# Summing the indexer's head scores on TensorE with diagonal weight matrices, and moving half of the queries behind the second selection

## Chip, cores and metric

The kernel runs on one core of one Trainium2 chip. The metric is the device time of one execution in microseconds (us); smaller is better. The inputs are float32, one sequence of 256 tokens of width 1024.

## What is computed

The program is a two-layer decoder trunk. Layer 0 uses a sparse latent attention: a small "indexer" scores every key for every query, the 64 best keys are kept, and eight heads attend over them. Layer 1 uses another attention (compressed blocks, selected blocks, a sliding window). Each layer ends in an MLP of width 4096. The change lies in the indexer and the attention of layer 0 alone:

```python
c_q, c_kv, k_idx, w_idx = split(h @ w_in, ...)         # 256, 128, 64, 8 columns; the first three normalised
q     = einsum('btr,rhd->bthd', c_q, w_uq)             # 8 heads of 128
q_abs = einsum('bthd,chd->bthc', q, w_uk) * HEAD_DIM ** -0.5
q_idx = einsum('btr,rhd->bthd', c_q, w_q_idx)          # 8 index heads of 64
rel   = relu(einsum('bqhd,bsd->bqhs', q_idx, k_idx))   # per index head
score = einsum('bqh,bqhs->bqs', w_idx, rel)            # weighted sum over the index heads
score = where(key_pos <= t, score, NEG)
_, sel = top_k(score, 64)
logits = einsum('bqhc,bqkc->bqhk', q_abs, c_kv[sel]) + rel_bias[...]
o_lat  = einsum('bqhk,bqkc->bqhc', softmax(logits), c_kv[sel])
```

## The kernel before

The 256 queries are two blocks of 128, `i` = 0 and 1. Block 0 sees 128 keys, block 1 sees 256. Queries lie on the 128 partitions, keys along the free dimension.

- **Index scores (lines 385 to 412).** `index_scores(i, m0)` multiplies the indexer's queries by the keys on TensorE in float32, two heads for each `m`, and ScalarE applies the relu into `rels[i]`.
- **Sum over heads (lines 461 to 466).** `score(i, n)` is one VectorE instruction: `rel` of head `n` times the head's weight `widx` (one value per query) plus the running sum. The first one adds the causal mask `cmask`. Eight of them make the score of one block.
- **Selection (lines 470 to 484).** `top8` finds the eight largest values of each row, `drop8` replaces them by a sentinel. Eight rounds of both mark 64 keys, and `select(i)` turns the marks into an additive mask `selm[i]`. All of these are VectorE instructions in an order written out by hand (`dve` is `inorder`, which puts each one behind the one before it on its engine).
- **Queries (lines 428 to 445).** `queries(hp)` makes the queries of a pair of heads. Each product is three TensorE passes over operands that are split into a high and a low half in fp32r (`mm3`); the halves of the weights are `wuq[j]`, where `j` = 0 holds heads 0 to 3 and `j` = 1 heads 4 to 7. The high half is a cast on ScalarE, the low half a subtraction on VectorE (line 379). `absorbed(hp)` multiplies by `w_uk` in float32.
- **Logits (lines 492 to 506).** `logits(i, h0)` computes two or four heads in one PSUM bank. `masked` adds `selm[i]` through a matmul with the identity, into the same bank. `exps`, `norms`, `transposed`, `values` and `upv` make the softmax and the mix; `wo_head` adds one head of the output projection `ya`.
- **Order.** The text of lines 677 to 772 gives the order in which work is issued. A scheduler may move an instruction ahead of others on its engine when its operands are ready; `pin` keeps an instruction in the order of the text, `behind` ties it to another one. Engine queues run in order. `Pieces` cuts a GpSimd operation into pieces of 256 columns and gives each piece an order; `load_wo(None, 0, 1)` loads the first two heads' output weights on the SP queue and splits them on GpSimd.
- **Buffers.** PSUM has two pools of four banks: `acc` (projections, logits, `ya`) and `ps` (everything else). `bigt` takes one of ten 8 KB slots per partition.

Of the kernel before, what the change touches and what calls it, by code (L numbers as in the profile page):

```python
# [22 lines left out]
F32 = mybir.dt.float32  # L23
F32R = mybir.dt.float32r
AF = mybir.ActivationFunctionType
OP = mybir.AluOpType
# [4 lines left out]
P, T, D, KT = 128, 256, 1024, 8  # L31
H, G, R, HD = 8, 2, 4, 128
# [18 lines left out]
def trunk(ctx: ExitStack, tc: tile.TileContext, I, out):  # L51
    nc = tc.nc
# [17 lines left out]
    def bank(name, acc=False):  # L70
        if acc:
            return psA.tile([P, 512], F32, tag="acc", name=name)
        return psB.tile([P, 512], F32, tag="ps", name=name)

    def bigt(shape, dt, name):
        return big.tile(shape, dt, tag="big", name=name)

    def wk(tag, bufs, shape, name, dt=F32):
        return work.tile(shape, dt, tag=tag, name=name, bufs=bufs)
# [10 lines left out]
    def f(ap):  # L90
        return ap.bitcast(F32)

    def mm(ps, a, b, start, stop):
        return nc.tensor.matmul(ps, a, b, start=start, stop=stop, skip_group_check=True)  # L94

    def mm3(ps, ah, al, bh, bl, start, stop):
        mm(ps, ah, bh, start, False)
        mm(ps, ah, bl, False, False)
        mm(ps, al, bh, False, stop)

    def behind(ins, prev):

        tc.add_manual_dep(ins.ins, prev.ins.name,
                          mybir.DependencyInfo(mybir.DependencyClass.NoSync, mybir.DependencyReason.DATA),
                          reason="order")
# [42 lines left out]
    def colw(src, name, m=P, lo=None, after=None, hi=None):  # L148
        h, l = weights(src, name, lo, after, hi)
        return (h.rearrange("p (k m) -> p k m", m=m), l.rearrange("p (k m) -> p k m", m=m))  # L150

    def pin(ins):

        return tc.keep_in_program_order(ins)
# [95 lines left out]
    for j in range(4):  # L250
# [8 lines left out]
        else:  # L259
            xh = nc.scalar.copy(xgh[:, pair], xT[:, pair])  # L260
            nc.vector.tensor_sub(xgl[:, pair], xT[:, pair], f(xgh[:, pair]))
            w = wp.tile([P, 2, 1024], F32R, tag="w", name=f"win{j}")
            wh, wl = (w[:, s, :912].rearrange("p (a m) -> p a m", a=2) for s in range(2))
            for a in range(2):
# [3 lines left out]
                                                         op0=OP.mult, op1=OP.subtract)  # L268
# [15 lines left out]
    ident = cst[:, C_ID:C_ID + P]  # L284
    cmask = cst[:, C_CM:C_CM + T]
# [8 lines left out]
    wuqr = [rawp.tile([P, 1024], F32, tag="raw", name=f"wuqr{j}") for j in range(2)]  # L294
# [45 lines left out]
    widx = const.tile([P, 2, H], F32, name="widx")  # L340
# [16 lines left out]
    sc = [scs[:, i] for i in range(2)]  # L357
    indexer_queries(0)
    tk = bank("tk")
    for i in range(2):  # L360
        kd = wk("kd", 2, [P, 2, 64], "kd")
        nc.vector.tensor_scalar(kd, proj[i][:, None, 384:448].to_broadcast([P, 2, 64]), sc[i][:, 2:3], None,
                                op0=OP.mult)
        pin(nc.tensor.transpose(tk[:, i * P:(i + 1) * P], kd.rearrange("p a b -> p (a b)"), ident))
    for a in range(2):
        pa = slice(64 * a, 64 * (a + 1))
        kiT_last = nc.vector.tensor_scalar(kiT[pa, a], tk[pa, :T], vec[pa, V_GKI:V_GKI + 1], None, op0=OP.mult)
    indexer_queries(1)
    for i in range(2):
        nc.vector.tensor_scalar(widx[:, i], proj[i][:, 448:456], sc[i][:, 3:4], float(8 ** -0.5 * 64 ** -0.5),  # L370
                                op0=OP.mult, op1=OP.mult)
        nc.vector.tensor_scalar(widx[:, i], widx[:, i], sc[i][:, 0:1], None, op0=OP.mult)
    wuq = []
    for j in range(2):
        w = wp.tile([P, 2, 1024], F32R, tag="w", name=f"wuq{j}")
        cast = nc.scalar.copy(w[:, 0], wuqr[j])
        behind(cast, cqu_last)
        behind(cast, ss_last)
        behind(nc.vector.tensor_sub(w[:, 1], wuqr[j], f(w[:, 0])), kiT_last)
        wuq.append((w[:, 0], w[:, 1]))  # L380


    rels = [bigt([P, 4, 2, (i + 1) * P], F32, f"rel{i}") for i in range(2)]

    def index_scores(i, m0):

        ns = (i + 1) * P
        per = 256 // ns
        ps = bank(f"ix{i}{m0}")
        for m in range(m0, m0 + per):  # L390
            for j in range(2):
                o = ((m - m0) * 2 + j) * ns
                pin(mm(ps[:, o:o + ns], qiT[:, m, i * P:(i + 1) * P], kiT[:, j, :ns], o == 0, o + ns == 512))
        return nc.scalar.activation(rels[i][:, m0:m0 + per].rearrange("p m j s -> p (m j s)"), ps, AF.Relu)
# [11 lines left out]
    for a in range(2):  # L406
# [1 line left out]
        nc.scalar.activation(cqs[:, 0, a], tn[:, a * T:(a + 1) * T], AF.Copy, scale=g)  # L408
        nc.vector.scalar_tensor_tensor(cqs[:, 1, a], tn[:, a * T:(a + 1) * T], g, f(cqs[:, 0, a]),
                                       op0=OP.mult, op1=OP.subtract)  # L410
    for m in range(4):
        rel_last = index_scores(1, m)
    tc_ = bank("tc")
    for i in range(2):
        nc.scalar.activation(ckv[:, i], proj[i][:, 256:384], AF.Copy, scale=sc[i][:, 1:2])
# [12 lines left out]
    def queries(hp):  # L428
        ps = bank(f"q{hp}")
        for a in range(2):  # L430
            h = 2 * hp + a
            for k in range(2):
                c = slice(k * 512 + (h % 4) * P, k * 512 + (h % 4 + 1) * P)
                wh, wl = wuq[h // 4]
                mm3(ps[:, a * T:(a + 1) * T], wh[:, c], wl[:, c], cqs[:, 0, k], cqs[:, 1, k],
                    k == 0 and a == 0, k == 1)
        qt_last.append(nc.scalar.copy(qT[:, 2 * hp:2 * hp + 2].rearrange("p a t -> p (a t)"), ps))

    def absorbed(hp):
        ps = bank(f"qa{hp}")  # L440
        for a in range(2):
            h = 2 * hp + a
            mm(ps[:, a * T:(a + 1) * T], wuk[:, h * P:(h + 1) * P], qT[:, h], a == 0, a == 1)
        qa_last.append(nc.scalar.activation(qabs[:, 2 * hp:2 * hp + 2].rearrange("p a t -> p (a t)"), ps, AF.Copy,
                                            scale=gkvs[:, 0:1]))
# [11 lines left out]
    dve = inorder  # L457

    scores = [wk("sq", 2, [P, T], f"score{i}") for i in range(2)]

    def score(i, n):
        ns = (i + 1) * P
        m, j = divmod(n, 2)
        prev = cmask[:, T - ns:] if n == 0 else scores[i][:, :ns]
        return dve(nc.vector.scalar_tensor_tensor(scores[i][:, :ns], rels[i][:, m, j], widx[:, i, n:n + 1], prev,
                                                  op0=OP.mult, op1=OP.add))

    m8s = {}

# [22 lines left out]
    def logits(i, h0, acc, first=False):  # L492
        ns = (i + 1) * P
        per = 512 // ns
        lg = bank(f"lg{i}{h0}", acc=acc)
        lg3 = lg.rearrange("p (a b) -> p a b", b=ns)
        for h in range(h0, h0 + per):
            ins = mm(lg3[:, h - h0], qabs[:, h, i * P:(i + 1) * P], ckvT[:, :ns], h == h0, False)
            if first and h == h0:
                pin(ins)  # L500
        return lg3

    def masked(i, lg3):
        ns = (i + 1) * P
        pin(mm(lg3, identr, selm[i][:, None, :ns].to_broadcast([P, 512 // ns, ns]), False, True))
        return lg3
# [144 lines left out]
    lg = {}  # L651
    wo = [None] * H

    def load_wo(prev, *hs):
        for h in hs:
            wo[h] = colw(I["a_w_o"][h], f"wo{h}", lo=pieces if h < 6 else nc.vector,
                         after=(prev,) if prev else None, hi=None if prev else pieces.tensor_copy)

    def past(prev):
        return lambda ins: after_sync(ins, prev)  # L660
# [13 lines left out]
        values(i, h0, pT[i, h0], ordered)  # L674


    for n in range(8):
        score(0, n)
    queries(0)
    queries(1)  # L680
    absorbed(0)
    absorbed(1)
    lg[0, 0] = logits(0, 0, True)
    for n in range(4):
        score(1, 2 * n)
        top8(0)
        score_last = score(1, 2 * n + 1)
        drop8(0)
    pieces = Pieces(past(score_last))
    queries(2)  # L690
    queries(3)
    for n in range(4):
        top8(1)
        top8(0)
        drop8(1)
        drop8(0)
    select(0)
    masked(0, lg[0, 0])
    load_wo(None, 0, 1)
    absorbed(2)  # L700
    absorbed(3)
    lg[0, 4] = logits(0, 4, True)
    masked(0, lg[0, 4])
    for h0 in (0, 2):
        lg[1, h0] = logits(1, h0, True, True)
    ex = exps(0, 0, True)
    for rnd in range(4):
        top8(1)
        if rnd in (1, 2):
            ex.pop(0)()  # L710
        drop8(1)
        if rnd in (1, 2):
            ex.pop(0)()
    select(1)
    for h0 in (0, 2):
        masked(1, lg[1, h0])
    lg[1, 4] = logits(1, 4, True, True)
    masked(1, lg[1, 4])
    def run(steps):
        for step in steps:  # L720
            step()
# [12 lines left out]
    pieces = Pieces(past(chains[mybir.EngineType.DVE][-1]))  # L734
# [44 lines left out]
    for fi in range(NF):  # L779
# [8 lines left out]
        if fi == 14:  # L788


            ps = bank("m1_ps")
# [41 lines left out]
    for k in range(KT):  # L833
# [5 lines left out]
        if k == 4:  # L839
            ms2 = small([P, 2], "ms2")  # L840
            ps = bank("ms2_ps")
# [30 lines left out]
    for kv in range(2):  # L872
        ps = bank(f"kc{kv}")
        for g in range(G):
# [4 lines left out]
        ins = nc.vector.tensor_tensor(ff[:, :, :32].rearrange("p b (g c) -> p b g c", g=G),  # L879
                                      ps.rearrange("p (g c b) -> p b g c", g=G, b=16),  # L880
                                      Rb.rearrange("p (c b) -> p b c", b=16)[:, :, None, :].to_broadcast([P, 16, G, 16]),
                                      op=OP.mult)
# [71 lines left out]
    for i in range(2):  # L954
        nc.scalar.activation(Vs[:, 0, i], vps[i], AF.Copy, scale=r2[:, i:i + 1])
        nc.vector.scalar_tensor_tensor(Vs[:, 1, i], vps[i], r2[:, i:i + 1], f(Vs[:, 0, i]),
                                       op0=OP.mult, op1=OP.subtract)
    gk = hidden(0, csk)
    kcT = const.tile([P, 32], F32, name="kcT")
    ps = bank("kcT_ps")  # L960
# [9 lines left out]
    w = wp.tile([P, 2, 1024], F32R, tag="w", name="wg")  # L970
# [190 lines left out]
    ps = bank("vc_ps")  # L1161
# [5 lines left out]
    for a in range(2):  # L1167
# [3 lines left out]
                                       op0=OP.mult, op1=OP.subtract)  # L1171
# [40 lines left out]
    for fi in range(NF):  # L1212
# [14 lines left out]
        if 16 <= fi < 20:  # L1227
            i, c = divmod(fi - 16, 2)
            ps = bank(f"x3t{i}{c}")
# [19 lines left out]
    for i in range(2):  # L1249
        for c in range(2):  # L1250
# [5 lines left out]
            if c == 0:  # L1256
                ins = nc.gpsimd.tensor_tensor(xg[:, i], x4[:, i, :512], gf[:, 0, :512], op=OP.mult)
# [4 lines left out]
        else:  # L1262
            for n in range(2):
                d = slice(512 + 256 * n, 768 + 256 * n)
                ps = bank(f"y11{n}")
# [121 lines left out]
```

## Time and profile before

| what | value |
|---|---|
| median of three runs | 593.86 us (593.1 to 595.12) |
| the profiled execution | 593.29 us |
| span of its trace | 591.5 us |
| PE busy | 577.2 us, 98% |
| PEld (weight loads) busy | 542.9 us, 92% |
| DVE busy | 364.2 us, 62% |
| ACT busy | 320.4 us, 54% |
| POOL busy | 159.1 us, 27% |

PE is TensorE's matmuls, PEld its weight loads (they overlap the matmuls), DVE is VectorE, ACT is ScalarE, POOL is GpSimd. The busy shares are means over the whole span. Matmuls are pipelined and the ends in the trace are modelled, so a busy PE can still have small holes between its instructions. The span is shorter than the time of the execution by what lies ahead of the first and behind the last instruction.

### The profile page before, as it was taken

How to read it: one execution, taken by the hardware profiler on the slowest of the kernel's cores; microseconds unless marked ns; L12 is line 12 of the kernel's file. 1: busy time of each engine (PE TensorE's matmuls, PEld its weight loads, DVE VectorE, ACT ScalarE, POOL GpSimd, SP SyncE). 2: the span in 40 equal slices, each digit the busy share in tenths (PEclk: the TensorE clock that was granted, in tenths of full speed). 3: DMA queues.
4: the chain of work that ended last, by engine and by line, in shares of the span. 5: the costliest groups of instructions: out<-in, count | busy, mean ns of one | idle time of the engine just before them, and what ended most of it. 6: DMA issues, size and time to landing. Idle time of an engine off the chain costs nothing.

```text
span 591.5 us, 10852 instructions
## 1 busy us (share of the span) xinstructions
PE 577.2 (98%) x4170; PEld 542.9 (92%) x4170; DVE 364.2 (62%) x612; ACT 320.4 (54%) x580; POOL 159.1 (27%) x225
## 2 busy tenths in 40 slices
PE   8899999999999999999999999999999999999995
PEld 6787899999999999999968999999899999999994
DVE  3897399544474444547897877639845444454523
ACT  6656666444444454436866878637544545454423
POOL 0155457010101011015530076808310110011012
PEclk9999999999999999999999999999999999999998
DMA  8911447765546656543499943314866665656201
GB/s 300 345 47 61 149 176 235 249 194 178 179 145 212 181 178 190 180 164 113 160 308 304 327 139 102 97 49 138 287 205 186 181 191 169 180 180 203 77 0 71
DMA packets 30475, 103.97 MB, mean 176 GB/s; under 512 B 3632, under 2 KB 5464, under 8 KB 30296
## 3 DMA queue, kind: packets, MB, share of 16 engines
q1 hardware_dynamic: 30024, 102.45, 53.7%
q10 hardware_dynamic: 400, 0.83, 0.5%
q8 instruction: 32, 0.52, 0.4%
q14 instruction: 19, 0.16, 0.1%
HBM read 102.21 MB, written 1.06 MB: 175 GB/s over the span
## 4 chain that ended last, share of the span: by engine, by line
PE 84%; DVE 9%; issue 2%; DMA 2%; ACT 1%; POOL 1%; SPq 1%; POOLq 0%; ACTq 0%; DVEq 0%
PE y L94 30%; PE u L94 28%; PE nq L94 4%; PE yb L94 3%; PE ya L94 3%; PE kk L94 2%; PE npo L94 2%; PE kc L94 1%; PE nl L94 1%; DVE c L903 1%; DMA win_raw<-in_a_w_in 1%; PE v L94 1%; PE co L94 1%; PE ix L94 1%; DMA wv_raw<-in_kvV 1%
## 5 line engine op out<-in xcount | busy, mean ns | idle before, releaser
L142 DVE TENSOR_TENSOR dn<-dn_raw,dn 128x1024 fp32r<-128x1024 f32 x64 | 80.6, 1260 | 99.2 <-ACT dn L141 99.2
L645 POOL TENSOR_TENSOR us<-ur 128x256 f32<-128x256 f32 x64 | 45.4, 711 | 282.0 <-ACT ur L642 282.0
L142 DVE TENSOR_TENSOR up<-up_raw,up 128x1024 fp32r<-128x1024 f32 x64 | 81.9, 1280 | 44.6 <-ACT up L141 44.6
L141 ACT CAST up<-up_raw 128x1024 fp32r<-128x1024 f32 x64 | 67.0, 1048 | 60.0 <-PE y L94 58.5
L94 PE MATMUL u<-h1h,up 128*128 128x256 f32 x512 | 97.0, 284 | 0.6 <-DVE up L142 0.6
L94 PE MATMUL y<-uu,dn 128*128 128x256 f32 x768 | 97.0, 283 | 0.3 <-DVE uu L647 0.3
L94 PE MATMUL u<-h0h,up 128*128 128x256 f32 x512 | 96.7, 283 | 0.0
L94 PEld LDWEIGHTS y<-uu,dn 128*128 128x128 f32 x768 | 94.2, 192 | 0.5 <-DVE uu L647 0.5
L94 PE MATMUL y<-dn,uu 128*128 128x512 f32 (+1 forms) x396 | 92.5, 384 | 0.0
L94 PEld LDWEIGHTS y<-dn,uu 128*128 128x128 f32 x396 | 71.1, 189 | 13.0
L94 PEld LDWEIGHTS u<-h1h,up 128*128 128x128 f32 x512 | 81.5, 191 | 1.6 <-DVE up L142 0.8
L642 ACT ACTIVATE ur<-u 128x256 f32<-128x256 f32 x64 | 24.6, 384 | 107.2 <-PE u L94 107.2
L94 PEld LDWEIGHTS u<-h0h,up 128*128 128x128 f32 x512 | 81.7, 192 | 0.0
L94 PE MATMUL u<-h1l,up 128*128 128x256 f32 x256 | 72.5, 283 | 0.0
L94 PE MATMUL u<-h0l,up 128*128 128x256 f32 x256 | 72.2, 283 | 0.0
L141 ACT CAST dn<-dn_raw 128x1024 fp32r<-128x1024 f32 x64 | 66.7, 1042 | 7.2 <-PE y L94 3.0
L94 PEld LDWEIGHTS u<-h1l,up 128*128 128x128 f32 x256 | 49.0, 191 | 0.9
L94 PEld LDWEIGHTS u<-h0l,up 128*128 128x128 f32 x256 | 49.1, 192 | 0.0
L647 DVE TENSOR_TENSOR uu<-us,uu 128x256 fp32r<-128x256 f32 x64 | 29.1, 455 | 8.1 <-POOL us L645 8.1
L646 ACT ACTIVATE uu<-ur 128x256 fp32r<-128x256 f32 x64 | 26.7, 417 | 0.1
L94 PE MATMUL ya<-oT,wo 128*128 128x256 f32 x192 | 25.2, 288 | 0.3 <-DVE oT L591 0.3
L94 PE MATMUL nq<-ah,wq 128*128 128x256 f32 x128 | 24.9, 286 | 0.0
(300 smaller groups left out, 966.8 us busy)
## 6 DMA issues: line engine op xcount, KB each, us to landing
up_raw<-in_w_up SPq DMA_DIRECT2D x64, 512.0 KB, 3.7
dn_raw<-in_w_down SPq DMA_DIRECT2D x64, 512.0 KB, 3.7
c1raw<-in_cmp_w SPq DMA_DIRECT2D x16, 512.0 KB, 4.9
wo_raw<-in_a_w_o SPq DMA_DIRECT2D x8, 512.0 KB, 4.1
wq_raw<-in_b_w_q SPq DMA_DIRECT2D x8, 512.0 KB, 5.9
wn_raw<-in_b_w_o SPq DMA_DIRECT2D x8, 512.0 KB, 4.9
wk_raw<-in_kvT SPq DMA_DIRECT2D x4, 512.0 KB, 3.6
wc_raw<-in_kvT SPq DMA_DIRECT2D x4, 512.0 KB, 3.6
```

Source lines behind the costliest of these rows:

```text
L94: return nc.tensor.matmul(ps, a, b, start=start, stop=stop, skip_group_check=True)
L141: ins = [hi(w[:, 0, :C], raw[:, :C]) if hi else nc.scalar.copy(w[:, 0, :C], raw[:, :C]), (lo or nc.vector).tensor_sub(w[:, 1, :C], raw[:, ...
L142: (lo or nc.vector).tensor_sub(w[:, 1, :C], raw[:, :C], f(w[:, 0, :C]))]
L642: nc.scalar.activation(r, ps[:, :T], AF.Relu)
L645: nc.gpsimd.tensor_tensor(s, r, r, op=OP.mult)
L646: nc.scalar.activation(u[:, 0], r, AF.Square)
L647: nc.vector.tensor_sub(u[:, 1], s, f(u[:, 0]))
L903: lo = nc.vector.tensor_sub(w4[:, :, 1], r4, f(w4[:, :, 0]))
```

## The change

The sum over the index heads becomes eight matmuls for each block. GpSimd builds `dg`, a 128x128 diagonal matrix for each block and head with the head's weights on the diagonal. `head_sums(i)` multiplies each by `rels[i]` of that head, in float32, and accumulates in one PSUM bank. `score(i)` is then one VectorE addition of the causal mask. The matmuls are pinned in between the index scores of block 1.

The order behind them changes too. `score(1)` stands behind three selection rounds of block 0. The logits of block 1 for heads 0 to 3 are written ahead of the selection; the queries, absorbed queries and logits of heads 4 to 7 stand behind the second selection. The low half of `wuq[1]` is subtracted on GpSimd, behind the diagonal matrices, and the first two output heads' weights are split behind that.

```diff
--- before.py
+++ after.py
@@ -376,8 +376,14 @@
         cast = nc.scalar.copy(w[:, 0], wuqr[j])
         behind(cast, cqu_last)
         behind(cast, ss_last)
-        behind(nc.vector.tensor_sub(w[:, 1], wuqr[j], f(w[:, 0])), kiT_last)
+        if j == 0:
+            behind(nc.vector.tensor_sub(w[:, 1], wuqr[j], f(w[:, 0])), kiT_last)
         wuq.append((w[:, 0], w[:, 1]))
+
+    dg = bigt([P, 2, H, P], F32, "dg")
+    for i in range(2):
+        dg_last = nc.gpsimd.tensor_tensor(dg[:, i], ident[:, None, :].to_broadcast([P, H, P]),
+                                          widx[:, i, :, None].to_broadcast([P, H, P]), op=OP.mult)
 
 
     rels = [bigt([P, 4, 2, (i + 1) * P], F32, f"rel{i}") for i in range(2)]
@@ -408,8 +414,19 @@
         nc.scalar.activation(cqs[:, 0, a], tn[:, a * T:(a + 1) * T], AF.Copy, scale=g)
         nc.vector.scalar_tensor_tensor(cqs[:, 1, a], tn[:, a * T:(a + 1) * T], g, f(cqs[:, 0, a]),
                                        op0=OP.mult, op1=OP.subtract)
-    for m in range(4):
-        rel_last = index_scores(1, m)
+    def head_sums(i):
+        ns = (i + 1) * P
+        ps = bank(f"sc{i}")
+        for n in range(H):
+            pin(mm(ps[:, :ns], dg[:, i, n], rels[i][:, n // 2, n % 2], n == 0, n == H - 1))
+        return ps
+
+    index_scores(1, 0)
+    index_scores(1, 1)
+    sums = [head_sums(0)]
+    index_scores(1, 2)
+    index_scores(1, 3)
+    sums.append(head_sums(1))
     tc_ = bank("tc")
     for i in range(2):
         nc.scalar.activation(ckv[:, i], proj[i][:, 256:384], AF.Copy, scale=sc[i][:, 1:2])
@@ -458,12 +475,9 @@
 
     scores = [wk("sq", 2, [P, T], f"score{i}") for i in range(2)]
 
-    def score(i, n):
+    def score(i):
         ns = (i + 1) * P
-        m, j = divmod(n, 2)
-        prev = cmask[:, T - ns:] if n == 0 else scores[i][:, :ns]
-        return dve(nc.vector.scalar_tensor_tensor(scores[i][:, :ns], rels[i][:, m, j], widx[:, i, n:n + 1], prev,
-                                                  op0=OP.mult, op1=OP.add))
+        return dve(nc.vector.tensor_tensor(scores[i][:, :ns], sums[i][:, :ns], cmask[:, T - ns:], op=OP.add))
 
     m8s = {}
 
@@ -674,48 +688,47 @@
         values(i, h0, pT[i, h0], ordered)
 
 
-    for n in range(8):
-        score(0, n)
+    score(0)
+
+    pieces = Pieces(lambda ins: behind(ins, dg_last))
+    pieces.tensor_sub(wuq[1][1], wuqr[1], f(wuq[1][0]))
+    load_wo(None, 0, 1)
     queries(0)
     queries(1)
     absorbed(0)
     absorbed(1)
     lg[0, 0] = logits(0, 0, True)
-    for n in range(4):
-        score(1, 2 * n)
+    for h0 in (0, 2):
+        lg[1, h0] = logits(1, h0, True)
+    for n in range(3):
         top8(0)
-        score_last = score(1, 2 * n + 1)
         drop8(0)
-    pieces = Pieces(past(score_last))
-    queries(2)
-    queries(3)
-    for n in range(4):
+    score(1)
+    for n in range(5):
         top8(1)
         top8(0)
         drop8(1)
         drop8(0)
     select(0)
     masked(0, lg[0, 0])
-    load_wo(None, 0, 1)
-    absorbed(2)
-    absorbed(3)
-    lg[0, 4] = logits(0, 4, True)
-    masked(0, lg[0, 4])
-    for h0 in (0, 2):
-        lg[1, h0] = logits(1, h0, True, True)
     ex = exps(0, 0, True)
-    for rnd in range(4):
+    for rnd in range(3):
         top8(1)
-        if rnd in (1, 2):
+        if rnd:
             ex.pop(0)()
         drop8(1)
-        if rnd in (1, 2):
+        if rnd:
             ex.pop(0)()
     select(1)
     for h0 in (0, 2):
         masked(1, lg[1, h0])
-    lg[1, 4] = logits(1, 4, True, True)
-    masked(1, lg[1, 4])
+
+    queries(2)
+    queries(3)
+    absorbed(2)
+    absorbed(3)
+    lg[0, 4] = masked(0, logits(0, 4, True))
+    lg[1, 4] = masked(1, logits(1, 4, True))
     def run(steps):
         for step in steps:
             step()
```

## Rows read from the trace of the kernel before

**Rows 1.** Busy by stretch: PE, PEld, DVE, ACT, POOL; then PEclk, DMA share, GB/s.
```profile
22.10:44.81 22.71, 21.86 (x138) 19.38 (x139) 22.20 (x86) 13.39 (x30) 8.49 (x17) 1.00 0.41 135
44.81:53.92 9.11, 8.47 (x39) 6.26 (x39) 5.61 (x23) 6.82 (x21) 3.18 (x9) 1.00 0.10 40
53.92:83.81 29.89, 29.89 (x226) 28.31 (x226) 19.93 (x39) 17.21 (x34) 15.78 (x22) 1.00 0.51 177
```

**Rows 2.** TensorE's groups by form, 22 to 54 us.
```profile
L94 PE MATMUL q<-cqs,wuq 128*128 128x256 f32 x48 | 6.8, 291 | 0.0
...
L94 PE MATMUL ix<-kiT,qiT 128*128 128x256 f32 x16 | 3.6, 379 | 0.0
L94 PE MATMUL lg<-selm,identr 128*128 128x512 f32 x6 | 2.9, 504 | 0.9 <-DVE selm L483 0.9
...
L94 PE MATMUL ix<-kiT,qiT 128*128 128x128 f32 x16 | 2.0, 278 | 0.0
...
L556 PE MATMUL tpa<-cst,pe 128*128 128x128 f32 x12 | 1.8, 272 | 0.0
...
L94 PE MATMUL po<-pT,ckv 128*128 128x512 f32 x2 | 1.1, 644 | 0.2 <-ACT pT L558 0.2
```

**Rows 3.** The chain that ended last: start us, us, what.
```profile
24.33 1.83 PE ix L94 x16
26.16 0.44 PE tn L404 x4
26.60 3.47 PE ix L94 x16
...
34.82 0.52 DVE m L472 x2
35.34 0.66 DVE score L476 x2
...
39.55 0.75 DVE selm L483
...
40.67 0.50 DVE score L476 x2
...
113.34 2.88 PE y L94 x24
```

**Rows 4.** TensorE's timeline, 38 to 46 us: start us, us, instructions.
```profile
38.54 1.97 PE L94 MATMUL qa<-qT,wukv 128*128 128x256 f32 x8
40.35 0.50 PE L94 MATMUL lg<-selm,identr 128*128 128x512 f32 x1
...
44.81 0.73 PE L94 MATMUL lg<-selm,identr 128*128 128x512 f32 x2 [0.85 <-DVE selm L483]
```

**Rows 5.** VectorE's groups by form, 22 to 45 us.
```profile
L465 DVE SCALAR_TENSOR_TENSOR score<-rel,widx,score 128x256 f32<-128x256 f32 x7 | 3.3, 473 | 0.0
...
L465 DVE SCALAR_TENSOR_TENSOR score<-rel,widx,score 128x128 f32<-128x128 f32 x7 | 2.4, 349 | 0.2
L379 DVE TENSOR_TENSOR wuq<-wuqr,wuq 128x1024 fp32r<-128x1024 f32 x2 | 2.4, 1220 | 0.0
```

**Rows 6.** GpSimd's groups, whole run; then one timeline row each of GpSimd and VectorE.
```profile
L123 POOL TENSOR_TENSOR wo<-wo_raw,wo 128x256 fp32r<-128x256 f32 x24 | 17.7, 777 | 4.2 <-ACT wo L141 4.2
L853 POOL TENSOR_TENSOR xns<-x,Rb 128x256 f32<-128x256 f32 x8 | 12.3, 1555 | 15.4 <-DVE al L160 11.5 <-DVE Rb L201 3.9
...
L1257 POOL TENSOR_TENSOR xg<-x,gf 128x512 f32<-128x512 f32 x2 | 2.6, 1305 | 6.1 <-DVE x L1240 6.1
...
21.54 0.70 POOL L356 TENSOR_TENSOR scs<-msx,mhalf 128x2 f32<-128x2 f32 x1
...
22.56 0.22 DVE L372 TENSOR_SCALAR widx<-widx,scs 128x8 f32<-128x8 f32 x1
```

**Rows 7.** ScalarE's groups by form, 22 to 54 us.
```profile
L444 ACT ACTIVATE qabs<-qa,gkvs 128x512 f32<-128x512 f32 x4 | 2.8, 689 | 1.1 <-PE qa L94 1.1
```

**Rows 8.** TensorE's weight loads by form, 22 to 54 us.
```profile
L94 PEld LDWEIGHTS ix<-kiT,qiT 128*128 128x128 f32 x32 | 5.0, 191 | 0.4
```

## Prediction

> **What bounds the kernel now.** The change touches the stretch between the indexer's queries and the first output projection, about 22 to 54 us, so the first view is the busy time by stretch. From 22.10 to 44.81 us TensorE shows 21.86 us busy of 22.71 and VectorE 22.20; from 44.81 to 53.92 TensorE shows 8.47 of 9.11 while VectorE falls to 5.61; from 53.92 to 83.81 TensorE is busy throughout [rows 1]. The granted clock is 1.00, that is 2.4 GHz, in all three. Two engines are full at once before 44.81, and TensorE alone after it.
>
> Busy rows of TensorE overlap and their ends are modelled, so the second view counts its instructions and the third gives their spacing. One float32 matmul shows as two records. The chain spaces 128-column float32 records by 1.83/16 = 0.114 us and 256-column ones by 3.47/16 = 0.217; 256-column fp32r records run at 2.88/24 = 0.12; transposes at 0.44/4 = 0.11 [rows 3]. Two fp32r records of 512 columns start 0.73 - 0.50 = 0.23 apart [rows 2, 4]; I give a 512-column float32 record twice 0.217. From 22.10 to 53.92 the trace has 68 float32 records of 256 columns (`ix` is one group of 16; `qi`, `lg`, `qa`, `po`, `ov` bring 52 more), 32 of 128 columns (`ix`, and 16 of `lg`), 50 fp32r (48 `q`, 2 `ya`), 20 transposes (12 `tpa`, 8 more), 6 masks and 2 of `po` with 512 columns [rows 2]. That is 14.76 + 3.65 + 6.0 + 2.2 + 1.38 + 0.86 = 28.85 us of work in 31.82 us. TensorE therefore has about 3.0 us of slack there: 1.49 that the stretches show as idle and 1.5 hidden between records. About 1.4 of the 3.0 lies before 44.81 and 1.6 behind it (39 records, 7.56 us).
>
> The chain itself runs through VectorE for most of the time before 44.81 us: scores, `max`, `match_replace`, the two masks, and TensorE waits 0.85 us for the second one [rows 3, 4]. A reader of the chain alone would call VectorE the bound. The stretch view says more: while VectorE selects, TensorE does work that has to be done anyway (queries and absorbed queries of heads 4 to 7).
>
> **The change part by part.** *VectorE.* Sixteen score steps go: eight of 128 columns at 0.349 and eight of 256 at 0.473, 6.6 us; one low half of the query weights goes, 1.22 us [rows 5]. Two additions from PSUM come. No row shows one; I price them like the same shapes, 0.35 and 0.47, with bounds of 0.2 (a 128-column `max` is spaced 0.26 [rows 3]) and 0.75 (the slowest 128-column row, `selm`). Net -7.0 us.
>
> *TensorE.* Sixteen float32 matmuls come: eight of 128 columns, 16 x 0.114 = 1.83 us, and eight of 256, 16 x 0.217 = 3.47. Nothing goes. Net +5.3 us, by the rate of the `ix` matmuls, which have the same shapes and types.
>
> *GpSimd.* Two products of 128x1024 come. The nearest rows are 1.305 us for 128x512 and 1.555 us for 128x256 beside busy VectorE [rows 6]: 2.6 us each at the low end, 4 x 1.555 = 6.2 at the high end. VectorE has only the 1.22 us subtraction and small work then, so I take 2.7. GpSimd is free from 22.2 us and the weights of block 0 are written at 22.8 [rows 6]; the products end near 25.6 and 28.3, ahead of the matmuls that read them (28.3 and 31.9 below). Behind them queue four pieces of the moved subtraction, 4 x 0.78 = 3.1 [rows 6], to 31.4; its readers, queries 2 and 3, come after 43. The first two output heads' splits queue next (16 pieces) and end near 40; `ya` reads them after 54. So this costs nothing in time while the queries stay late. The loads' place in the SP queue does not change; one raw buffer comes free some 5 us later, for an output weight not needed before 54.
>
> The Trainium skill's page "SBUF — State Buffer" (on engine ports) has VectorE operations with two SBUF inputs and GpSimd operations that read SBUF lock each other out entirely, which speaks against putting the products beside the remaining subtraction. By that rule one of the two starts up to 2.7 us later; the products still end by 29.6 and VectorE is idle until 30.3 anyway, so the sum stays, and its hard form is the late-GpSimd rival below.
>
> *The order.* TensorE from 24.33: `ix` for block 0 to 26.16, `tn` 0.44, half of `ix` for block 1 to 28.33, sums of block 0 to 30.16, the other half to 31.9, sums of block 1 to 35.4. VectorE: score 0 at about 30.3, three lone rounds for block 0 to 32.8 (0.65 to 0.7 each, below the 0.87 of a lone 256-column round [rows 3]), then the in-order queue waits for the second sums: everything behind `score(1)` stands, the rest of both selections. Score 1 ends at 36.0. Five double rounds of 0.52 + 0.66 take 5.9, to 41.9; the first mask 0.75, to 42.65; three more rounds with four softmax steps 3.6 (before, four took 4.46 from 40.30, and one is 0.87) [rows 3]. The second mask ends at 46.2, not 44.76: 1.45 us later although VectorE has 7 us less to do.
>
> TensorE from 35.4 to 46.2 has `tc`, all four queries, two absorbed, three `logits` and a mask: 0.22 + 5.76 + 1.73 + 0.92 + 1.73 + 0.23 = 10.6 us. That fills the wait if queries 2 and 3 are hoisted over the masks that the text puts ahead of them. Before, `qa` of heads 4 to 7 runs at 38.54, ahead of the mask at 40.35 that is written earlier [rows 4], so such hoisting occurs. From 46.2 remain the 7.56 us of before plus what moved behind: two absorbed 1.73, `lg` 0.92 and its mask 0.23, together 10.4. Dense, that ends at 56.6 to 56.7 instead of 53.92. ScalarE takes over two `qT` and two `qabs` copies there, at most 4 x 0.689 = 2.8 us [rows 7], on top of its 6.82; that and the handovers from `pe` to `oT` leave some slack, of which I keep 0.8. Shift: 57.5 - 53.92 = 3.6 us. From 53.92 on TensorE has no idle time in which to win it back [rows 1].
>
> As a balance: 5.3 us added, less slack used up. With all 3.0 used the loss is 2.3; with none, 5.3. The value 3.6 keeps 1.3.
>
> The profiled execution took 593.29 us, 1.79 more than its span, and the median is 593.86. On the profile's footing the forecast is 596.9; on the median's, 597.4. A difference of less than 0.3% (1.8 us) can't be told from no change here.
>
> **Rivals.** *The sums hide.* TensorE's limit is not the spacing but something with room. Weight loads are busy 19.38 + 6.26 = 25.64 us of 31.82, so 6.2 are free, and the new 32 loads take 32 x 0.191 = 6.1 [rows 1, 8]. Then only the later selection shows: 593.86 + 1.45 = 595.3, no change. Against it: in the MLP 0.191 us loads sit behind matmuls spaced 0.12, so loads overlap each other, and spacing follows columns [rows 3, 8]. The Trainium skill's "Perfetto Trace Analysis" (Identifying the Most-Contended Engine) calls matmul busy time a bad measure and wants the share of weight loads; that is this rival. The trace agrees on the first half only. Chance 0.13.
>
> *VectorE's 7 us count: faster.* If the sums take almost no TensorE time, score 1 comes right behind `ix` at about 31.5 and the second mask at 41.7, 3.0 us earlier; TensorE's work, 28.85 us from 22.10, then ends at 50.95: 593.86 - 3.0 = 590.9. The chain's VectorE stretch speaks for it. It decides once the sixteen matmuls cost less than the 3.0 us of slack; `ix` of equal shape costs 5.3. Chance 0.07.
>
> *GpSimd late: slower still.* At 6.2 us a product the second ends at 35.3 and the sums of block 1 start 3.4 us late, with the selection behind them: 600.9. For it: the 1.555 us rows. Against: VectorE's light load then. The same size comes if the hoisting fails and TensorE stands until 46.2. Chance 0.14.
>
> **How the numbers follow.** The forecast case has 0.66, with its own range 596.2 (all slack used) to 599.2 (none). The range leaves out the faster case and the far end of the late one: 595.0 to 600.5. Faster 0.07; within 0.3% 0.13; slower 0.66 + 0.14 = 0.80.
>
> **What would show it.** Right: `sc` matmuls of 1.8 and 3.5 us in TensorE's timeline and no idle time there to 35 us; VectorE idle for 2 to 3 us ahead of `score(1)`; the second `selm` near 46; first `ya` block near 57; the shift unchanged at 84 us and at the end. Wrong: `sc` records closer than 0.11 and 0.21 us, a second `selm` ahead of 44, or GpSimd rows for `dg` over 4 us. A different order of instructions behind 97 us, where the stretches are not worked out here, could add or hide 1 us.

## The result and the profile after

The changed kernel takes 598.22 us in the median of five runs (596.61 to 599.19), the kernel before 593.86: ratio 1.0073, 95% interval 1.0049 to 1.0097. It is slower by 4.4 us; the forecast was 597.4, in a range of 595.0 to 600.5. The span of the profiled execution grew by the same 4.4 us, from 591.5 to 595.9.

The busy time by stretch: from the first `tk` matmul to 44.81 us as in [rows 1], from there to the start of the full block of `ya`, and some 30 us behind it, with columns PE, PEld, DVE, ACT, POOL, granted clock, DMA share and GB/s:

```profile
22.08:44.81 22.73, 22.73 (x148) 21.04 (x148) 14.75 (x56) 9.54 (x19) 15.89 (x23) 1.00 0.44 151
44.81:58.38 13.57, 12.87 (x64) 9.42 (x63) 7.92 (x37) 10.25 (x32) 3.01 (x9) 1.00 0.00 0
58.38:88.37 29.99, 29.99 (x225) 28.26 (x226) 20.02 (x39) 17.15 (x34) 15.88 (x22) 1.00 0.52 176
```

TensorE now shows no idle time at all before 44.81 us, where it had 0.85. VectorE falls from 22.20 busy to 14.75. The second stretch ends at 58.38 instead of 53.92, and the third is as long as before and as full. So the time is lost ahead of `ya` and nothing behind gives it back: from the block of `ya` to the end of the trace it is 591.5 - 53.92 = 537.6 us before and 595.9 - 58.38 = 537.5 after.

TensorE's timeline (start us, us, instructions):

```profile
22.08 0.50 PE L364 MATMUL tk<-cst,kd 128*128 128x128 f32 x2 [0.72 <-DVE kd L362]
...
39.81 2.50 PE L94 MATMUL q<-cqs,wuq 128*128 128x256 f32 x18
...
46.16 0.58 PE L94 MATMUL lg<-selm,identr 128*128 128x512 f32 x1
...
49.17 1.02 PE L94 MATMUL lg<-ckvT,qabs 128*128 128x256 f32 x4
...
58.38 4.21 PE L94 MATMUL ya<-oT,wo 128*128 128x256 f32 x33 [0.28 <-DVE oT L605]
```

and the two ends of the same stretch in the kernel before:

```profile
22.10 0.50 PE L364 MATMUL tk<-cst,kd 128*128 128x128 f32 x2 [0.71 <-DVE kd L362]
...
53.92 4.21 PE L94 MATMUL ya<-oT,wo 128*128 128x256 f32 x33 [0.28 <-DVE oT L591]
```

From the first `tk` matmul to the full block of `ya` it is 58.38 - 22.08 = 36.30 us; before, 53.92 - 22.10 = 31.82. This distance grew by 4.48 us. It is the measure for the experiments too, because the start of `tk` moves by up to 2.1 us between traces with what runs ahead of it.

The chain that ended last (start us, us, what) no longer runs through VectorE's selection. It runs through the new matmuls:

```profile
28.31 1.78 PE sc L94 x16
30.09 1.73 PE ix L94 x8
31.82 1.73 PE sc L94 x8
33.55 0.22 PE tc L433 x2
33.76 0.87 PE sc L94 x4
34.63 0.95 PE q L94 x8
35.58 0.86 PE sc L94 x4
...
40.17 2.15 PE q L94 x18
...
58.38 4.21 PE ya L94 x33
```

Block 0's sums take 1.78 us and block 1's 1.73 + 0.87 + 0.86 = 3.46, together 5.24. The spacing is that of `ix` in [rows 3]. Block 1's sums are cut in two places: the scheduler put `tc` and eight records of `q` in between, 1.17 us, so they end at 36.4.

VectorE's timeline, the rows that wait or that end a selection:

```profile
23.69 1.07 DVE L372 TENSOR_SCALAR widx<-widx,scs 128x8 f32<-128x8 f32 x1
24.67 1.21 DVE L380 TENSOR_TENSOR wuq<-wuqr,wuq 128x1024 fp32r<-128x1024 f32 x1
...
30.13 0.29 DVE L480 TENSOR_TENSOR score<-sc,cst 128x128 f32<-128x128 f32 x1 [1.17 <-PE sc L94]
...
36.48 0.43 DVE L480 TENSOR_TENSOR score<-sc,cst 128x256 f32<-128x256 f32 x1 [3.91 <-PE sc L94]
...
42.94 0.23 DVE L497 TENSOR_SCALAR selm<-score 128x128 fp32r<-128x128 f32 x1
...
46.78 0.29 DVE L536 CUSTOM_DVE_ANT_0 pe<-lg,biasT 128x128 f32<-128x128 f32 x1 [2.29 <-PE lg L94]
...
48.74 0.29 DVE L497 TENSOR_SCALAR selm<-score 128x256 fp32r<-128x256 f32 x1
```

`score(1)` waits 3.91 us for the sums. The first mask is ready at 43.2, but VectorE then stands 2.29 us, because TensorE has other work ahead of the mask matmul and reaches it only at 46.16: 24 records of `q` hoisted from heads 4 to 7 (18 of them in one go at 39.81), 16 of logits and 4 of `qa`. The second mask ends at 49.03; before, TensorE received it at 44.81 [rows 4].

GpSimd's groups between 22 and 40 us:

```profile
L385 POOL TENSOR_TENSOR dg<-cst,widx 128x1024 f32<-128x1024 f32 x2 | 4.7, 2350 | 0.7 <-DVE widx L372 0.6
...
L123 POOL TENSOR_TENSOR wuq<-wuqr,wuq 128x256 fp32r<-128x256 f32 x4 | 2.8, 726 | 0.0
```

The same two products with the shortest, the middle and the longest time in ns:

```profile
L385 POOL TENSOR_TENSOR dg<-cst,widx x2: 1897/2350/2802, 22.8 to 24.8; 128x1024 f32<-128x1024 f32 x2
```

The diagonal matrices take 2.35 us in the mean, 1.90 for the first and 2.80 for the second, and end at 27.6, ahead of their readers. The moved subtraction keeps the pace of its kind.

### The profile page after: what moved, and what is told of

Read it like the earlier page. It is cut to its first block, busy times and chain, and to the rows that moved or that the text cites. A ratio compares the mean times of both kernels' runs of the same rounds, so it can differ in the third digit from the quotient of the medians.

```text
span 595.9 us, 10908 instructions
## 1 busy us (share of the span) xinstructions
PE 582.1 (98%) x4202; PEld 547.6 (92%) x4202; DVE 358.9 (60%) x597; ACT 319.8 (54%) x580; POOL 166.6 (28%) x231
## 4 chain that ended last, share of the span: by engine, by line
PE 87%; DVE 6%; DMA 2%; issue 2%; ACT 2%; POOL 1%; SPq 1%; POOLq 0%; ACTq 0%; DVEq 0%
PE y L94 30%; PE u L94 28%; PE nq L94 4%; PE yb L94 3%; PE ya L94 3%; PE kk L94 2%; PE npo L94 2%; PE kc L94 1%; PE nl L94 1%; PE co L94 1%; PE lg L94 1%; PE v L94 1%; DMA win_raw<-in_a_w_in 1%; PE q L94 1%; DMA wv_raw<-in_kvV 1%
## 5 line engine op out<-in xcount | busy, mean ns | idle before, releaser
L94 PEld LDWEIGHTS ya<-oT,wo 128*128 128x128 f32 x192 | 23.8, 191 | 1.2 <-DVE oT L605 0.5
```

## The experiments

Two theories stand against each other. **Theory 1**, that of the prediction: the 5.3 us of float32 matmuls are work on an engine that is full, and the loss is this work less the slack it uses up. **Theory 2**: the new order is the loss; the queries of heads 4 to 7 get ahead of the first mask, and the selection ends over 4 us later. All runs had five rounds beside the kernel before; the ratio is to that kernel in the same rounds.

| run | from `tk` to `ya`, us | median, us | ratio (95%) |
|---|---|---|---|
| before | 31.82 | 593.86 | |
| changed | 36.30 | 598.22 | 1.0073 (1.0049 to 1.0097) |
| e1_order_only | 37.16 | 599.23 | 1.0089 (1.0072 to 1.0105) |
| e2_sums_old_order | 36.27 | 598.38 | 1.0073 (1.0054 to 1.0092) |
| e3_sums_fp32r | 32.90 | 594.28 | 1.0002 (0.9994 to 1.0011) |
| e4_sums_twice | 41.39 | 603.02 | 1.0148 (1.0129 to 1.0167) |
| e5_wuq_gpsimd | 31.74 | 592.85 | 0.9989 (0.9978 to 1.0) |
| e6_block0_only | 33.02 | 594.32 | 1.0015 (1.0005 to 1.0026) |
| e7_queries_moved | 31.45 | 593.43 | 0.9994 (0.9983 to 1.0005) |
| e8_queries_held | 36.37 | 597.69 | 1.0064 (1.0048 to 1.0079) |
| e9_fp32r_old_order | 32.39 | 593.60 | 0.9997 (0.9986 to 1.0009) |
| e10_order_interleaved | 34.97 | 596.05 | 1.0041 (1.0028 to 1.0055) |
| e11_splits_held | 31.42 | 593.11 | 0.9994 (0.9982 to 1.0007) |

Each distance comes from one traced execution. In e3 it is 1.08 us longer than before, while the ratio allows at most 0.65 us; so a few tenths of distance are not yet time.

**e2_sums_old_order: the sums alone.** The kernel before with `dg`, `head_sums` and the short `score` of the change. The order behind them is that of the kernel before; four selection rounds of block 0 stand ahead of `score(1)`.

```diff
+    score(0)
+    pieces = Pieces(lambda ins: behind(ins, dg_last))
+    pieces.tensor_sub(wuq[1][1], wuqr[1], f(wuq[1][0]))
     queries(0)
...
     for n in range(4):
-        score(1, 2 * n)
         top8(0)
-        score_last = score(1, 2 * n + 1)
         drop8(0)
+    score_last = score(1)
     pieces = Pieces(past(score_last))
```

> The sums stay on TensorE with the diagonal matrices and the subtraction on GpSimd; the order of everything behind them is that of the kernel before. Theory 1: 597 to 599, as the changed kernel, because the work is the same. Theory 2: 595 or less.

It took 598.38 us and 36.27 from `tk` to `ya`, the changed kernel's numbers within 0.2 us. Theory 1. The new order is not needed for the loss. The second mask of e2 ends at 49.03, on a trace whose `tk` starts at 23.69:

```profile
48.74 0.29 DVE L498 TENSOR_SCALAR selm<-score 128x256 fp32r<-128x256 f32 x1
```

That is 25.34 us behind `tk`, 1.6 us earlier than the 26.95 of the changed kernel, and yet the distance to `ya` is the same.

**e7_queries_moved: the new place of the queries alone.** The sums stay on VectorE (as in e1, an earlier run that comes last here), with score steps and selection steps in pairs as before.

```diff
     lg[0, 0] = logits(0, 0, True)
+    for h0 in (0, 2):
+        lg[1, h0] = logits(1, h0, True)
...
-    queries(2)
-    queries(3)
...
     for h0 in (0, 2):
         masked(1, lg[1, h0])
+    queries(2)
+    queries(3)
+    absorbed(2)
+    absorbed(3)
+    lg[0, 4] = masked(0, logits(0, 4, True))
+    lg[1, 4] = masked(1, logits(1, 4, True))
```

> The kernel before, with VectorE's score steps interleaved with the selection as they were, and only the queries, absorbed queries and logits of heads 4 to 7 written behind the second selection. The order alone run had its eight score steps of block 1 in one block at 0.63 us each and TensorE's clock fell, so it was no clean test. Theory 1 (matmul work): the work is that of before, 593 to 595, 31.8 us from the first tk matmul to the first full block of ya. Theory 2 (moving the queries costs): 597 or more.

593.43 us: no change from before. The scheduler hoists most of the queries to where they were: the group of 18 records of heads 4 to 7 starts 12.5 us behind `tk` in both kernels, the last six 0.8 to 2.1 us later than before. Their place in the text costs nothing.

**e3_sums_fp32r and e4_sums_twice: the same program with less and more of the suspected work.**

```diff
-    dg = bigt([P, 2, H, P], F32, "dg")
+    dg = bigt([P, 2, H, P], F32R, "dg")
...
-    rels = [bigt([P, 4, 2, (i + 1) * P], F32, f"rel{i}") for i in range(2)]
+    rels = [bigt([P, 4, 2, (i + 1) * P], F32R, f"rel{i}") for i in range(2)]
```

```diff
-        for n in range(H):
-            pin(mm(ps[:, :ns], dg[:, i, n], rels[i][:, n // 2, n % 2], n == 0, n == H - 1))
+        for n in range(2 * H):
+            pin(mm(ps[:, :ns], dg[:, i, n // 2], rels[i][:, n // 4, n // 2 % 2], n == 0, n == 2 * H - 1))
```

> The changed kernel with diagonal matrices and relu outputs rounded to fp32r, so that each sum matmul is one pass: 8 x 0.06 + 8 x 0.12 = 1.4 us instead of 5.3. Theory 1: 3.9 us less work, 594 to 595. Theory 2: the order is unchanged, so 596.5 or more. If weight loads were what counts, 16 fewer of 0.19 us would give about 595 as well, which the doubled sums then tell apart.

> The changed kernel with each of the sixteen sum matmuls issued twice into the same accumulation, which doubles every score and leaves the order of the keys as it was. Theory 1: 5.3 us more work against at most 2.15 us of slack left between 22.08 and 58.38 us: 601.4 to 603.5. Theory 2: 598 to 600, since the late first mask leaves room in which more sums hide.

The sums in the chain, first with rounded operands (block 0, then block 1 in three parts):

```profile
28.58 0.84 PE sc L94 x8
...
31.20 0.47 PE sc L94 x4
...
31.89 0.24 PE sc L94 x2
...
33.56 0.24 PE sc L94 x2
```

and issued twice:

```profile
28.29 3.57 PE sc L94 x32
...
33.59 3.45 PE sc L94 x16
...
37.26 3.46 PE sc L94 x16
```

With rounded operands they take 0.84 + 0.95 = 1.8 us, 3.45 less than in the changed kernel, and the distance from `tk` to `ya` falls by 36.30 - 32.90 = 3.40. The expectation had 1.4: a 128-column record in fp32r takes 0.84/8 = 0.105 us, nearly as long as a float32 one, and not half of a 256-column one (0.95/8 = 0.119). Issued twice they take 10.5, 5.24 more, and the distance grows by 5.09. In both directions the distance follows the matmul work almost one to one. Of the further 5.24 us only 0.15 was hidden, although the changed kernel still had 2.15 of slack.

Columns and weight loads are told apart by the changed kernel itself. The sums of both blocks have 16 records and 16 loads, and block 1's, with twice the columns, take 3.46 us against 1.78.

**e9_fp32r_old_order** joins the edits of e2 and e3.

> Sums on TensorE with operands rounded to fp32r (1.4 us instead of 5.3) and the order of the kernel before. Theory 1: work 30.3 us against 31.8 before from tk to ya, so between 592.8 (slack falls by half) and 594.3 (as the same sums in the new order). If the new order cost anything, this is over 1 us below the fp32r run in the new order.

It came to 593.60, inside the first range and 0.7 us under e3. The intervals of the two overlap, so this run can't tell whether the order costs a few tenths.

**e6_block0_only: the cheap third of the sums.** Block 0's sums on TensorE, block 1's on VectorE; the low half of `wuq[1]` on GpSimd; the rest as before.

```diff
+    for m in range(4):
+        rel_last = index_scores(1, m)
+        if m == 1:
+            sums = [head_sums(0)]
...
+        if i == 0:
+            return dve(nc.vector.tensor_tensor(scores[0][:, :ns], sums[0][:, :ns], cmask[:, T - ns:], op=OP.add))
```

> The kernel before with only the sums of block 0 on TensorE (8 x 0.229 = 1.83 us) and the low half of the second query weights on GpSimd; block 1 keeps its eight VectorE steps and the order stays. VectorE loses 2.8 + 1.2 - 0.3 = 3.7 us. Theory 1: 1.83 us of work less what an earlier selection frees of the 3.0 us of slack: 594 to 595.5. If VectorE's chain set the end, 590.5 to 592.

594.32 us, slower than before by 0.15% (0.05 to 0.26). The added 1.83 us lengthen the distance by 1.20. VectorE had 3.7 us less to do, and the time did not fall. This alone does not clear VectorE's chain: block 1's index scores now stand behind the sums, its score steps start later, and the second mask ends 23.59 us behind `tk` instead of 22.65. e2 and e8 separate the two.

**e5_wuq_gpsimd: only the subtraction moved.** The kernel before with the low half of `wuq[1]` on GpSimd.

```diff
-        behind(nc.vector.tensor_sub(w[:, 1], wuqr[j], f(w[:, 0])), kiT_last)
+        if j == 0:
+            behind(nc.vector.tensor_sub(w[:, 1], wuqr[j], f(w[:, 0])), kiT_last)
+        else:
+            Pieces(lambda ins: None).tensor_sub(w[:, 1], wuqr[j], f(w[:, 0]))
```

> The kernel before with one edit: the low half of the second query weights subtracted on GpSimd, 1.2 us less for VectorE ahead of the selection. Theory 1 (TensorE's work sets the end): within 0.5 us of 593.8, since the 0.85 us wait for the second mask is all that can go. If VectorE's chain set the end: 592.5.

592.85 us, ratio 0.9989 with an interval that ends at 1.0, and 31.74 us from `tk` to `ya` against 31.82. The forecasts were within 0.5 us of 593.8 and 592.5; the median lies between them, 0.6 us below that of its own rounds. The interval, 0 to 1.3 us of gain, holds both, so this run does not decide.

**e8_queries_held: the late mask mended.** The changed kernel, with the first matmul of queries 2 and 3 tied behind the first mask.

```diff
+                ins = mm(qs, wh[:, c], cqs[:, 0, k], first, False)
+                if first and hp > 1:
+                    behind(ins, mask_last[0])
```

> The changed kernel with the first matmul of queries 2 and 3 tied behind the first mask, so that they no longer run ahead of the logits and the mask that VectorE waits 2.3 us for. Theory 1: VectorE is early but TensorE has the same 34.15 us of work and 2.15 of slack, at best 1 us less, more likely 597.5 to 599. Theory 2 (the late mask sets the end): 595.5 to 596.

VectorE's rows show the mend: the first mask's matmul follows at once and the second mask ends at 46.43, 2.6 us earlier than in the changed kernel (2.4 counted from `tk`).

```profile
42.73 0.23 DVE L503 TENSOR_SCALAR selm<-score 128x128 fp32r<-128x128 f32 x1
...
46.14 0.29 DVE L503 TENSOR_SCALAR selm<-score 128x256 fp32r<-128x256 f32 x1
...
53.27 0.69 DVE L580 COPY pT<-tpa 128x512 f32<-128x512 f32 x1 [2.29 <-PE tpa L578]
```

Yet the distance is 36.37 us and the time 597.69, as in the changed kernel. The wait comes back as 2.29 us of VectorE ahead of `pT`. The chain of e8 shows what stands there instead:

```profile
46.43 0.58 ACT qT L460
47.01 0.39 ACT pe L548 x2
47.40 0.58 ACT qabs L467
47.98 1.17 ACT pe L564 x4
49.15 0.98 ACT pe L548 x4
50.13 0.58 ACT qabs L467
...
50.76 2.04 PE lg L94 x10
```

From 46.43 to 50.71 it is ScalarE: three copies of the late queries (`qT`, `qabs`) in between the steps of the softmax (`pe`). The late mask was real, and taking it away gained nothing: the second mask ends 24.56 us behind `tk` in e8, 25.34 in e2 and 26.95 in the changed kernel, and the distance to `ya` is 36.3 to 36.4 in all three, with the same TensorE work. That ScalarE's copies take over the end is read from the chain; no run moves them.

**e1_order_only, e10_order_interleaved, e11_splits_held: the part that surprised.** e1 undoes the sums and keeps everything else, the early splits of the first output weights on GpSimd among it; block 1's eight score steps stand in one block.

```diff
-    score(0)
+    for n in range(8):
+        score(0, n)
...
-    pieces = Pieces(lambda ins: behind(ins, dg_last))
+    pieces = Pieces(lambda ins: None)
...
-    score(1)
+    for n in range(8):
+        score(1, n)
```

> The head sums go back to sixteen VectorE steps; the new order and the subtraction on GpSimd stay. Theory 1 (5.3 us of added matmul work on a full TensorE, less the slack it uses, is the loss): back to 593.9 within 1 us, first ya block near 54 us. Theory 2 (the new order is the loss: queries of heads 4 to 7 run ahead of the first mask and the selection ends 4 us late): stays at 597 or more, the second mask near 49 us.

It was the slowest of all that add no work, 599.23 us, with the second mask at 49.25. On its face that is what Theory 2 expects, and Theory 1 does not explain it. e10 puts the score steps back in pairs around the selection steps:

```diff
-    for n in range(3):
-        top8(0)
-        drop8(0)
-    for n in range(8):
-        score(1, n)
+    for n in range(4):
+        score(1, 2 * n)
+        if n:
+            top8(0)
+        score(1, 2 * n + 1)
+        if n:
+            drop8(0)
```

> The order-only kernel again (sums on VectorE, new order, subtraction on GpSimd), with the eight score steps of block 1 put in pairs around the selection steps of block 0 as in the kernel before, instead of in one block. If the block of dependent steps (0.63 us each against 0.39) and the clock that fell behind it made that run slow: 593 to 594.5, granted clock 1.0 throughout. If the new order or the subtraction on GpSimd did: 597 or more.

596.05 us: neither of the two outcomes. VectorE's group of score steps in e10, from 30.4 to 37.3 us (count, then busy time and mean ns):

```profile
L466 DVE SCALAR_TENSOR_TENSOR score<-rel,widx,score 128x256 f32<-128x256 f32 x7 | 4.7, 676 | 0.1
```

A step takes 676 ns where [rows 5] have 473, and GpSimd splits output weights beside it until 35.6 us. e11 holds those splits back until the last score step, as the kernel before does with `past(score_last)`; the loads of these weights move in the text with them:

```diff
-    pieces = Pieces(lambda ins: None)
-    pieces.tensor_sub(wuq[1][1], wuqr[1], f(wuq[1][0]))
-    load_wo(None, 0, 1)
+    Pieces(lambda ins: None).tensor_sub(wuq[1][1], wuqr[1], f(wuq[1][0]))
...
+    pieces = Pieces(past(score_last))
+    load_wo(None, 0, 1)
```

> The interleaved order-only kernel with the splits of the first two output weights held back on GpSimd until the last score step, as the kernel before holds them; the queries' weights are still subtracted there at once. If GpSimd's splits beside VectorE's score steps (0.68 to 0.87 us against 0.47) made the two order-only runs slow: score steps back at 0.47, no TensorE wait over 1 us, granted clock 1.0 and 592.5 to 594. If the new order did: 595.5 or more.

```profile
L466 DVE SCALAR_TENSOR_TENSOR score<-rel,widx,score 128x256 f32<-128x256 f32 x7 | 3.3, 473 | 0.1
```

The steps are back at 473 ns, TensorE's longest wait between `tk` and `ya` is 0.33 us, and the time is 593.11, no change from before. e11 keeps the new order, so the order as such is not the loss. So in e10 the early splits slowed VectorE, the selection came late, TensorE ran dry, and its clock fell on top of that. e1 has the same splits; its block of eight steps was not tried without them, so what the block adds stays open. TensorE's wait in e10, and the stretches that show the last step:

```profile
43.58 0.50 PE L94 MATMUL lg<-selm,identr 128*128 128x512 f32 x1 [2.35 <-DVE selm L484]
```

```profile
41.20:43.60 2.40, 0.04 (x2) 0.02 (x1) 2.37 (x14) 0.69 (x1) 0.00 (x0) 1.00 0.00 0
43.60:44.40 0.80, 0.80 (x4) 0.70 (x5) 0.75 (x3) 0.00 (x0) 0.00 (x0) 1.00 0.00 0
...
45.50:47.00 1.50, 1.38 (x6) 1.24 (x6) 1.49 (x10) 1.49 (x8) 0.00 (x0) 0.50 0.00 0
47.00:48.00 1.00, 1.00 (x3) 0.84 (x3) 0.18 (x1) 0.76 (x4) 0.00 (x0) 0.50 0.00 0
...
48.50:50.00 1.50, 1.45 (x9) 1.03 (x8) 0.91 (x5) 0.78 (x4) 0.00 (x0) 1.00 0.00 0
```

After a wait of 2.35 us TensorE resumes at 43.58 with the clock still granted in full; from about 45 to 48 us it is at 0.50, the lower of its two levels, 1.2 GHz.

## Why the prediction was right, and by how much it was off

- **TensorE is full, and the sums are plain added work.** Priced at 5.3 us, measured 5.24. The rate of `ix` was the right row. e3, e4 and e6 change this work, and the distance follows it. The second mask moves with it in those runs, so a later selection alone could do the same; e2 and e8 rule that out, where the mask ends 1.6 and 2.4 us earlier at the same work and the distance stays.
- **The slack left was mis-sized.** I kept 0.8 us behind the second mask, 1.3 in the balance. The changed kernel kept 36.30 - (28.85 + 5.3) = 2.15, so it used 0.85 of the 3.0, not 1.7. The shift was 4.48 us instead of 3.6. The error lies behind the second mask. From 49.17 to `ya` stand the same 39 records as before behind 44.81, 9.21 us of time for 7.56 of work, against 9.11: these 1.6 us of slack stayed whole, where I kept 0.8. I had counted the absorbed queries and logits of heads 4 to 7 among the work there (10.4 us); with the mask so late, they ran ahead of it.
- **The selection is later although VectorE has less to do.** Right in its direction; forecast 46.2 for the second mask, measured 49.0. Block 1's sums end 1 us later, as queries are hoisted into them, and the first mask waits 2.3 us behind hoisted queries. I had the hoisting as a gain alone; it has this price too. But e8 takes the price away (its second mask ends at 46.43, near the forecast) and gains nothing on the distance from `tk` to `ya`, so it explains the late mask and not the shift. That the total came near all the same is no proof of the path that was forecast.
- **GpSimd.** 1.90 and 2.80 us for the products against 2.7 taken for each, and the readers did not wait. By the Trainium skill's "SBUF — State Buffer" (Who interferes with whom), where a GpSimd operation and a VectorE operation want the ports that the two engines share, the first to start keeps them for its whole instruction and the other waits. The trace agrees, in both directions: the 8-column `widx` write of 23.69, 0.22 us in [rows 6], takes 1.07 and ends where the first product does, at 24.7; and the second product, which starts at 24.8 beside the subtraction that runs on VectorE until 25.88, takes 0.90 longer than the first. It cost nothing, as forecast.
- **"The early splits cost nothing."** True in the changed kernel, for a reason that I did not give: its VectorE has no score steps left beside them. e2 holds the splits back and takes the same time. With the score steps on VectorE the same edit costs 2.9 us of median (e10 against e11, whose runs of before are 0.25 us apart).
- **Rivals.** *The sums hide* falls with e4: 32 more weight loads and 5.24 us of columns cost 5.09. *VectorE's 7 us count* falls with the changed kernel's own rows: the sums take 5.24 us, more than all the slack, and the second mask ends at 49.0 and not at 41.7. *GpSimd late* did not happen. Theory 2 falls with e2, e7, e8 and e11.
- **Time behind `ya`.** No part of the shift was won back by 88 us, as forecast.

None of the versions run here beats the kernel before clearly; e5 comes nearest.

## What to carry to other kernels

Where two engines are full in the same stretch, look at what each is full of: VectorE's chain here was long but covered TensorE work that had to be done anyway, so moving VectorE's sums onto TensorE only added to the engine that sets the end. Count that engine's records at their spacing and compare with the stretch; the difference is all that a change there can hide, and much of it may not be usable: here 0.85 of 3.0 us was, and the slack behind the last mask was not touched. Before releasing work on GpSimd early, look at which VectorE instructions with two inputs in SBUF will run beside it.

## What the runs showed of the hardware that was not expected

- A VectorE score step of 128x256 with both tensor inputs in SBUF takes 676 ns in the mean beside GpSimd's splits (e10) and 473 without (e11). The `max` and `match_replace` steps beside the same splits keep their 282 and 271 ns (e10). The splits' subtractions slow down too, from 731 ns in the mean (e11) to 859 (e10). This agrees with the lock-out that the Trainium skill's "SBUF — State Buffer" (Who interferes with whom) describes for VectorE operations with two SBUF inputs.
- A wait of TensorE of 2.35 us, after a stretch in which it was busy throughout, was followed by some 3 us at 0.50 of the clock, and they began only after TensorE was at work again (e10). The 0.85 us wait of the kernel before left the clock at 1.00 [rows 1]. In e1, waits of 1.67 and 2.18 us with some 1.2 us of work between them were followed by 0.50 from about 48 to 54.6 us, which began within the second wait.
